# A decoder layer on one core: own tensors in memory for each gated tile, the first half of the merged values kept on chip, residual rows asked for later, the two steps of a norm set apart

## The chip, the core and the metric

The kernel runs on one core of a Trainium2 chip. The core has a matrix engine (PE, with its weight loads shown as PEld), three engines for elementwise work (DVE, ACT, POOL), a queue engine SP that does nothing but ask for transfers, and 16 DMA engines that move the bytes. POOL asks for some transfers too; SP's and POOL's requests go through two different queues (q1 and q0 of the profile). Each engine works its own list of instructions in order and waits at an instruction until everything that it needs is there. The metric is device time in microseconds (us) of one execution; the profile's span runs from the first to the last instruction.

## The reference

One step of a decoder layer over 1024 prompt tokens and 8 sample tokens, in float32. Cut to what matters:

```
def swiglu_half(x, g, w_gate, w_up, w_down):
    u = rmsnorm(x, g)
    return x + 0.5 * ((jax.nn.silu(u @ w_gate) * (u @ w_up)) @ w_down)

h = swiglu_half(x, ...)                        # block one, D_MODEL 1024, D_FF 2816
u = rmsnorm(h); z = u @ w_in                   # latent attention, retention, two gates
h = h + w_out(sigmoid(g_A) * (A @ w_branch_att) + sigmoid(g_B) * (B @ w_branch_ret))
h = swiglu_half(h, ...)                        # block two
h = h + sigmoid(rmsnorm(h) @ w_ple_gate) * (p @ w_ple_proj)
```

The value in the bracket that goes into `w_out` is called the merged value below; silu(gate) times up is called the gated value.

## The kernel before

**Tiling.** All activations lie with features on the 128 partitions and tokens along the free axis. The 1032 tokens are cut into two halves (`tp` 0 and 1) of 2 x 258; `lr` names one 258 of a half. Float32 is multiplied as a high and a low part, three matmuls per product (lines 138 to 140, 331 to 334, 378 to 380, 556 to 558). `split` (lines 103 and 104) makes the parts: a cast on ACT, a subtraction on DVE. KT = 8 is the number of feature tiles of D_MODEL, NF = 22 that of D_FF.

**Stages in order of time.** Block one: norm, gate and up products (to 478 us), down product (493 to 754). Then retention and gates, attention (to 1512). Then the merge: 32 units of 12 matmuls (`proj`, lines 138 to 140), one per feature tile, half and `lr`. Then the out product (`product`, wm times wout). Then block two with the same code as block one (its down product from 2153), and the final part.

**The gated values.** `Block.run` computes gated tiles; `put` splits them and writes each to the memory tensor `mid_d[f, tp]` (SP, line 535; 22 tiles for each half). At the end `fetch` (line 691) asks for the 22 tiles of the first half back from POOL's queue, later for those of the second half from SP's. `product` then runs over the 22 tiles, eight banks at once, 24 matmuls a tile. The rows `h` of the residual stream (line 699, 1032 KB) are added to the product's result when a pass over the 22 tiles is over; that of the first pass is asked for on POOL's queue, the others on SP's. Weight slices `wd` come through SP (line 311).

**The norm.** `rstd2` sums squares with small matmuls over the partitions (line 349), takes a reciprocal root in three rounds on DVE (line 351 and lines 143 to 147, results `sv`, `st`, `sz`), yields, then spreads the result over the partitions (matmuls of line 358, copy to `r` in line 360). At the start of a block `run` asks for four pairs of gate and up products (`plain`, lines 556 to 558); the norm of a half is done between the gate product and the up product of its first pair.

**The merge.** Each unit multiplies its product with a gate `sg` (line 1436), adds the other branch `mr` (line 1437), splits the sum into `mst`, and after two units SP writes 516 KB of `mst` to `mg_d[o, tp]` (line 1442). `sg` and `mr` are asked for five units ahead (line 1417). At unit 20 the code opens the list of wout slices (`Rows`, line 311, 128 KB a slice), asks for the eight merged tiles of the first half back as `wm` (`operand(0)`, line 1403) and for that half's rows of the residual `ht` (`residual(0)`, line 1407, two loads of 1032 KB). After the first group of the out product come `operand(1)` and `residual(1)` for the second half. Results go out through line 1465.

**What sets the order.** The code's own order is not the final one: a planner sorts the instructions of each engine when the program is built, and each waits for what it needs, so that a load can stand earlier on its queue than its line suggests. The rows under "The change" show the final lists.

Of the kernel before, what the change touches and what calls it, by code (L numbers as in the profile page):

```python
# [10 lines left out]
F32 = mybir.dt.float32  # L11
F32R = mybir.dt.float32r
# [8 lines left out]
P = 128  # L21
D = 1024
KT = D // P
# [6 lines left out]
NF = DFF // P  # L30
# [26 lines left out]
def body(ctx, tc, a):  # L57
# [27 lines left out]
    act.copy(warm, ones[:, 0:1])  # L85
    G_QA, G_KVA, G_RET = 5 * KT, 5 * KT + 2, 5 * KT + 3

    hs_d = drp.tile([P, KT, T], F32, name="hs_d")
    h2_d = drp.tile([P, KT, T], F32, name="h2_d")
    h3_d = drp.tile([P, KT, T], F32, name="h3_d")  # L90
    mid1_d = drp.tile([NF, 2, P, 2, 2 * HC], F32, name="mid1_d")
    mid2_d = drp.tile([NF, 2, P, 2, 2 * HC], F32, name="mid2_d")
    ms_d = drp.tile([KT, P, T], F32, name="ms_d")
    ga_d = drp.tile([KT, P, T], F32, name="ga_d")
    u1_d = drp.tile([KT, P, 2, 2 * HC], F32, name="u1_d")
    u2_d = drp.tile([KT, P, 2, 2 * HC], F32, name="u2_d")
    mg_d = drp.tile([KT, 2, P, 2, 2 * HC], F32, name="mg_d")
    vs_d = drp.tile([NB, RH * RD], F32, name="vs_d")


# [142 lines left out]
    def both(tp):  # L243
        return slice(2 * tp * HC, 2 * tp * HC + 2 * HC)

    class Stream:
# [26 lines left out]
        def make(self, units):  # L273
            r = self.load(*units[0])
            self.early(r)
            for i in range(len(units)):
                nxt = None
                for q, part in zip(ORDER, ("a11", "s1", "a11", "a12", "a21", "a12", "a22")):
                    yield self.split(r[part])
                    if q == 0:  # L280
                        dve.tensor_tensor(r["a11"], r["s1"], r["a11"], op=ALU.subtract)
                        if i + 1 < len(units):
                            nxt = self.load(*units[i + 1])
                    elif q == 3:
                        dve.tensor_tensor(r["a12"], r["a12"], r["a11"], op=ALU.subtract)
                    elif q == 6 and nxt:
                        self.early(nxt)
                r = nxt

        def take(self):  # L290
            while len(self.ready) <= self.ahead:
# [130 lines left out]
    class Block:  # L422
# [100 lines left out]
        def run(self, nxt, nxt_st, prepare, accs=None, load=None, more=None):  # L523
# [38 lines left out]
                return self.pe.tile([P, HC], F32, tag="p", name="p")  # L562

            for n, (l, tp) in enumerate(((0, 0), (1, 0), (1, 1), (0, 1))):
                if n == 0 and not begun:
                    rows.ahead, ws, pg = 0, [], []
                    for lr in range(2):
                        load(0, lr)
                        self.fresh(0, lr)
                        ws += [rows.take() for _ in range(2)]  # L570
                        pg.append(plain(ws[:2], 0, lr))
                    load(1, None)
                    squared(0)
                    rows.ahead = 3
                else:
                    if n != 2:
                        ws = [rows.take() for _ in range(4)]
                    pg = [plain(ws[:2], tp, lr) for lr in range(2)]
                if n in (0, 2) and accs[tp] is not None:
                    for _ in self.norm(tp, accs[tp]):  # L580
                        pass
                pu = [plain(ws[2:], tp, lr) for lr in range(2)]
                ts = []
                for lr in range(2):
                    t = pt()
                    ts.append(t)
                    dve.tensor_tensor(t, pg[lr][:, :HC], self.r[tp][:, HV[lr]], op=ALU.mult)
                    act.activation(t, t, AF.Silu)
                for lr in range(2):
                    dve.tensor_tensor(ts[lr], pu[lr][:, :HC], ts[lr], op=ALU.mult)  # L590
                    put(0, tp, l, lr, ts[lr])
                if n == 0:
                    if not begun:
                        squared(1)
                    for _ in self.plain_tokens(1):
                        pass
                elif n == 1:
                    if not begun:
                        self.scaled(0)
                        for _ in self.sums(0):  # L600
                            pass
                    self.last_sum(0)
                elif n == 2:
                    for _ in self.sums(1):
                        pass
# [83 lines left out]
            def fetch(tp, f):  # L689
                mids[tp, f] = t = mp.tile([P, 2, 2 * HC], F32R, tag="m", name="m")  # L690
                self.loaded = (sp if tp else pool).dma_start(t.bitcast(F32), self.mid_d[f, tp])
# [3 lines left out]
            with pools(pre + "h", 2) as hp, pools(pre + "t", 2) as tmp:  # L695
                for tp in TPS:
                    for o in range(2):
                        ht = hp.tile([P, 4, 2 * HC], F32, tag="h", name="h")
                        (sp if tp or o else pool).dma_start(ht, self.src[:, 4 * o:4 * o + 4, both(tp)])
                        end = tp == 1 and o == 1  # L700
                        if end:
                            next(nxt.norms[0])
                        banks = product(rows, lambda f: mids[tp, f], NF, 4,
                                        (lambda f: fetch(1, f)) if (tp, o) == (0, 1) else None)
                        if tp == 1 and o == 0:
                            with tc.issue_after(self.loaded.ins):
                                nxt.first = prepare(nxt.ring)
                        if end:
                            m_st.close()
                            nxt.open_u(nxt_st)  # L710
                            nxt.fetch()
                            next(nxt.norms[0])
                        for n in range(8):
                            hv = ht[:, n // 2, HV[n % 2]]
                            t = tmp.tile([P, HC], F32, tag="c", name="c")
                            dve.scalar_tensor_tensor(t, banks[n][:, :HC], 0.5, self.r[tp][:, HV[n % 2]],
                                                     op0=ALU.mult, op1=ALU.mult)
                            dve.tensor_tensor(hv, hv, t, op=ALU.add)
                            if n % 2:
                                k = 4 * o + n // 2  # L720
                                sp.dma_start(self.dst[:, k:k + 1, both(tp)], ht[:, n // 2:n // 2 + 1])
                        if tp == 1 and o == 0:
                            held = ht
                        if end:
                            for k in range(4):
                                nxt.row(tmp, 1, k, held[:, k])
                        for k in range(4):
                            if tp == 0 or end:
                                nxt.row(tmp, tp, 4 * o + k, ht[:, k])
                        for k in range(4):  # L730
                            nxt.squares(tmp, tp, 4 * o + k, ht[:, k], dve if end else pool)
                        if end and more:
                            more()
# [663 lines left out]
    wms = [wm_st.enter_context(pools("wm0", KT))]  # L1397
    xs = {}

    def operand(tp):  # L1400
        for f in range(KT):
            xs[tp, f] = t = wms[tp].tile([P, 2, 2 * HC], F32R, tag="wm", name="wm")
            sp.dma_start(t.bitcast(F32), mg_d[f, tp])

    def residual(tp):
        for k in range(0, KT, 4):
# [2 lines left out]
    with pools("mt", 2) as mt:  # L1409
# [14 lines left out]
        for j, (tp, o, lr) in enumerate(todo):  # L1424
            if j + 5 < len(todo):
                fetch(*todo[j + 5])
            if j == 20:
                rows = Rows(two.wp, two.rawp, [a["wout"][f][:, o_ * 256:o_ * 256 + 256]
                                               for _ in TPS for o_ in range(4) for f in range(KT)], 3)
                operand(0)  # L1430
                residual(0)
            sg, mr = gates.pop((tp, o, lr))
            ps = bank()
            proj(ps[:, :HC], wa[o // 2], oat, cols(tp, lr), off=(o % 2) * 512)
            m = mt.tile([P, HC], F32, tag="m", name="m")
            dve.tensor_tensor(m, ps[:, :HC], sg, op=ALU.mult)
            dve.tensor_tensor(m, m, mr, op=ALU.add)
            if lr == 0:
                st = mt.tile([P, 2, 2 * HC], F32R, tag="mst", name="mst", bufs=4)
            split(st[:, 0, HV[lr]], st[:, 1, HV[lr]], m)  # L1440
            if lr == 1:
                sp.dma_start(mg_d[o, tp], st.bitcast(F32))
    oat_st.close()
    ring_st.close()

# [4 lines left out]
    for tp in TPS:  # L1450
        sums_of.append(two.accs())
        for o in range(4):
# [2 lines left out]
                    next(steps, None)  # L1455
            banks = product(rows, lambda f: xs[tp, f], KT, 2, each)
            if tp == 0 and o == 0:
                operand(1)
                residual(1)
            for n in range(4):  # L1460
                k = 2 * o + n // 2
# [231 lines left out]
```

## Time and profile before

| what | us |
|---|---|
| three runs, median (lowest to highest) | 2559.3 (2559.25 to 2562.37) |
| the profiled execution's own time | 2556.08 |
| its span | 2553.4 |
| PE busy in the span | 2455.3 (96%) |
| PE's wait ahead of block one's down product | 14.4 |
| PE's wait ahead of block two's down product | 14.6 |
| PE's wait for the norm of block one's second half | 5.4 |
| PE's waits between 1557 and 1612 us, merge and out product | 23.1 |

PE is busy nearly all the time, so the table is to be read from the waits: each line below the fourth is a place where PE stood still, and the line of the code that it stood before is given in the views that are shown with the prediction. The PEclk column there is the mean clock that PE was granted, 1.00 being full.

### The profile page before, as it was taken

The numbers are of one execution on the slowest core, as the hardware profiler recorded it, in microseconds if no ns is written. First come the engines' busy times: TensorE is split into PE (matmuls) and PEld (weight loads), VectorE is DVE, ScalarE is ACT, GpSimd is POOL, SyncE is SP. The second block draws the span as 40 slices with busy tenths as digits, with TensorE's granted clock in tenths as the row PEclk, the third lists the DMA queues.
The fourth block names the chain that finished last, engine by engine and source line by source line (L and its number), as shares of the span: only waits on it lengthen the run. The fifth ranks groups of instructions, "written<-read, shape, count | busy, mean of one in ns | idle before, by whom it ended". The sixth has DMA issues, their size and how long they took to land.

```text
span 2553.4 us, 48889 instructions
## 1 busy us (share of the span) xinstructions
PE 2455.3 (96%) x19132; PEld 2364.0 (93%) x19132; DVE 1473.8 (58%) x3408; ACT 959.8 (38%) x2099; POOL 184.4 (7%) x247
## 2 busy tenths in 40 slices
PE   7999999799999999999999998899999997999998
PEld 7999999799999999999976677899999997999997
DVE  8767667533534666422567774676676675344345
ACT  7444444322322112211245552454444443233221
POOL 0000000111001101110142100000000001110011
PEclk9999999899999999999999998899999998999999
DMA  4323233759622122222134349543232337596231
GB/s 163 104 84 117 103 107 125 268 210 323 206 102 82 56 68 81 82 81 88 38 99 123 113 129 348 184 133 104 84 117 98 111 125 265 204 326 205 92 121 67
DMA packets 176168, 353.15 MB, mean 138 GB/s; under 512 B 19337, under 2 KB 69922, under 8 KB 175938
## 3 DMA queue, kind: packets, MB, share of 16 engines
q1 hardware_dynamic: 163938, 311.08, 36.1%
q0 software_dynamic: 12000, 38.96, 4.1%
q8 instruction: 150, 2.46, 0.4%
q14 instruction: 80, 0.66, 0.1%
HBM read 257.11 MB, written 91.80 MB: 137 GB/s over the span
## 4 chain that ended last, share of the span: by engine, by line
PE 89%; DMA 4%; DVE 4%; issue 1%; ACT 1%; SPq 1%; POOLq 0%; POOL 0%; DVEq 0%; ACTq 0%
PE ps L333 11%; PE ps L331 10%; PE ps L334 10%; PE ps L378 8%; PE ps L379 7%; PE ps L380 7%; PE ps L138 7%; PE ps L139 7%; PE ps L140 7%; PE ps L1186 2%; PE ps L1211 1%; PE ps L1222 1%; PE ps L556 1%; PE ps L557 1%; PE ps L558 1%
## 5 line engine op out<-in xcount | busy, mean ns | idle before, releaser
L333 PE MATMUL ps<-b,w 128*128 128x258 f32 x2240 | 636.6, 284 | 0.0
L331 PE MATMUL ps<-b,w 128*128 128x258 f32 x2240 | 633.1, 283 | 0.0
L334 PE MATMUL ps<-b,w 128*128 128x258 f32 x2240 | 630.2, 281 | 0.0
L378 PE MATMUL ps<-m,w 128*128 128x258 f32 x1408 | 402.6, 286 | 30.7 <-DMA m<-mid_d 29.1
L334 PEld LDWEIGHTS ps<-b,w 128*128 128x128 f32 x2240 | 427.0, 191 | 0.0
L333 PEld LDWEIGHTS ps<-b,w 128*128 128x128 f32 x2240 | 424.8, 190 | 0.0
L331 PEld LDWEIGHTS ps<-b,w 128*128 128x128 f32 x2240 | 421.5, 188 | 0.0
L379 PE MATMUL ps<-m,w 128*128 128x258 f32 x1408 | 399.4, 284 | 0.0
L380 PE MATMUL ps<-m,w 128*128 128x258 f32 x1408 | 398.7, 283 | 0.0
L104 DVE TENSOR_TENSOR w<-wd,w 128x512 fp32r<-128x512 f32 (+1 forms) x264 | 164.8, 637 | 300.1 <-ACT w L103 286.0
L138 PE MATMUL ps<-u,w 128*128 128x344 f32 (+4 forms) x960 | 311.9, 325 | 2.7 <-DMA u<-u_d 2.7
L139 PE MATMUL ps<-u,w 128*128 128x344 f32 (+4 forms) x960 | 308.1, 321 | 0.0
L140 PE MATMUL ps<-u,w 128*128 128x344 f32 (+4 forms) x960 | 307.6, 320 | 0.0
L378 PEld LDWEIGHTS ps<-m,w 128*128 128x128 f32 x1408 | 267.8, 190 | 32.5 <-issue 14.8
L103 ACT CAST w<-wd 128x512 fp32r<-128x512 f32 (+1 forms) x264 | 147.8, 566 | 365.1 <-PE ps L380 325.1
L379 PEld LDWEIGHTS ps<-m,w 128*128 128x128 f32 x1408 | 269.2, 191 | 0.0
L380 PEld LDWEIGHTS ps<-m,w 128*128 128x128 f32 x1408 | 268.1, 191 | 0.0
L104 DVE TENSOR_TENSOR w<-wq,w 128x512 fp32r<-128x512 f32 x264 | 181.5, 689 | 147.9 <-ACT w L103 145.6
L138 PEld LDWEIGHTS ps<-u,w 128*128 128x128 f32 (+1 forms) x960 | 180.1, 188 | 5.4 <-DVE u L413 2.7
L139 PEld LDWEIGHTS ps<-u,w 128*128 128x128 f32 (+1 forms) x960 | 179.5, 187 | 0.9 <-issue 0.4
L140 PEld LDWEIGHTS ps<-u,w 128*128 128x128 f32 (+1 forms) x960 | 179.7, 187 | 0.6
L103 ACT CAST w<-wq 128x512 fp32r<-128x512 f32 x264 | 163.5, 620 | 32.4 <-PE ps L334 23.6
(320 smaller groups left out, 4163.9 us busy)
## 6 DMA issues: line engine op xcount, KB each, us to landing
mid_d<-s SPq DMA_DIRECT2D x88, 516.0 KB, 3.6
m<-mid_d POOLq DMA_DIRECT2D x44, 516.0 KB, 12.3
m<-mid_d SPq DMA_DIRECT2D x44, 516.0 KB, 4.7
wd<-in_f1down_dram SPq DMA_DIRECT2D x88, 256.0 KB, 5.0
wd<-in_f2down_dram SPq DMA_DIRECT2D x88, 256.0 KB, 3.8
ct<-in_cache_dram SPq DMA_DIRECT2D x128, 128.0 KB, 2.1
wq<-in_f1gate_dram SPq DMA_DIRECT2D x44, 256.0 KB, 4.5
wq<-in_f1up_dram SPq DMA_DIRECT2D x44, 256.0 KB, 2.6
```

The lines of the kernel that those rows point to most:

```text
L103: act.copy(dst_hi, src)
L104: dve.tensor_tensor(dst_lo, src, dst_hi.bitcast(F32), op=ALU.subtract)
L138: pe.matmul(ps, w[:, 0, ws], x[:, 0, xs], start=start, stop=False)
L139: pe.matmul(ps, w[:, 0, ws], x[:, 1, xs], start=False, stop=False)
L140: pe.matmul(ps, w[:, 1, ws], x[:, 0, xs], start=False, stop=stop)
L331: pe.matmul(ps, w[:, 0, js], t[:, 0], start=q in (0, 1, 3) and j == 0, stop=False, skip_group_check=True)
L333: pe.matmul(ps, w[:, 0, js], t[:, 1], start=False, stop=False, skip_group_check=True)
L334: pe.matmul(ps, w[:, 1, js], t[:, 0], start=False, stop=j == kh - 1, skip_group_check=True)
L378: pe.matmul(ps, w[:, 0, ws], t[:, 0, HV[n % 2]], start=f == 0, stop=False)
L379: pe.matmul(ps, w[:, 0, ws], t[:, 1, HV[n % 2]], start=False, stop=False)
L380: pe.matmul(ps, w[:, 1, ws], t[:, 0, HV[n % 2]], start=False, stop=f == nf - 1)
L1186: pe.matmul(ps[:, :w], qc[hd][:, i * P:(i + 1) * P], kc[hd][:, j:j + w], start=True, stop=not diag)
```

## The change

Four edits:

- Each gated tile has its own tensor in memory (`halves`, 44 tensors for each block) in place of one tensor for all.
- The rows `h` are all asked for on SP's queue, in the code from inside the product (at its fifth tile).
- The merged values of the first half are split directly into the `wm` tiles that the out product reads; they are no longer written to memory and read back. Only the second half's eight tiles go through memory, each in its own tensor. The wout list is opened at unit 16; at units 25, 27, 29 and 31 one more slice is split ahead (`ahead_one`); `residual(0)` stands behind the merge loop.
- In the first four pairs the norm's first step (sums and root) and its second (spreading) are set apart: for the second half the sums now stand ahead of the gate product, and the spreading always behind the up product.

```
-    mid1_d = drp.tile([NF, 2, P, 2, 2 * HC], F32, name="mid1_d")
+    def halves(name, n):
+        return {(i, tp): drp.tile([P, 2, 2 * HC], F32, name=f"{name}{i}_{tp}") for i in range(n) for tp in range(2)}
+    mid1_d = halves("mid1_d", NF)
...
-    mg_d = drp.tile([KT, 2, P, 2, 2 * HC], F32, name="mg_d")
+    mg_d = [drp.tile([P, 2, 2 * HC], F32, name=f"mg_d{i}") for i in range(KT)]
...
+        def ahead_one(self):
+            self.ready.append(next(self.made))
...
+                norm = None
+                if n == 2 and accs[tp] is not None:
+                    norm = self.norm(tp, accs[tp])
+                    next(norm)
...
-                if n in (0, 2) and accs[tp] is not None:
-                    for _ in self.norm(tp, accs[tp]):
-                        pass
+                if n == 0 and accs[tp] is not None:
+                    norm = self.norm(tp, accs[tp])
+                    next(norm)
                 pu = [plain(ws[2:], tp, lr) for lr in range(2)]
+                if norm:
+                    next(norm)
...
-                        (sp if tp or o else pool).dma_start(ht, self.src[:, 4 * o:4 * o + 4, both(tp)])
+                        def each(f):
+                            if f == 4:
+                                sp.dma_start(ht, self.src[:, 4 * o:4 * o + 4, both(tp)])
+                            if (tp, o) == (0, 1):
+                                fetch(1, f)
...
-            if j == 20:
+            if j == 16:
                 rows = Rows(two.wp, two.rawp, [a["wout"][f][:, o_ * 256:o_ * 256 + 256]
                                                for _ in TPS for o_ in range(4) for f in range(KT)], 3)
-                operand(0)
-                residual(0)
+            elif j > 24 and j % 2:
+                rows.ahead_one()
...
             if lr == 0:
-                st = mt.tile([P, 2, 2 * HC], F32R, tag="mst", name="mst", bufs=4)
+                if tp == 0:
+                    xs[0, o] = st = wms[0].tile([P, 2, 2 * HC], F32R, tag="wm", name="wm")
+                else:
+                    st = mt.tile([P, 2, 2 * HC], F32R, tag="mst", name="mst", bufs=4)
             split(st[:, 0, HV[lr]], st[:, 1, HV[lr]], m)
-            if lr == 1:
-                sp.dma_start(mg_d[o, tp], st.bitcast(F32))
+            if tp == 1 and lr == 1:
+                sp.dma_start(mg_d[o], st.bitcast(F32))
+    residual(0)
```

**SP at the start of block one's down product.** Line 535 (541 in the changed kernel) writes gated tiles, line 699 (714) asks for `h`, line 311 (317) for weight slices. Before:

```order
51 L311 DMA wd<-in_f1down_dram 128x512 x13
52 L535 DMA mid_d<-s 128x1032 x2
53 L311 DMA wd<-in_f1down_dram 128x512
54 L699 DMA h<-in_xT_dram 128x4x516
55 L311 DMA wd<-in_f1down_dram 128x512 x20
```

Now:

```order
81 L317 DMA wd<-in_f1down_dram 128x512 x13
82 L541 DMA mid_d_0_114<-s 128x1032
83 L541 DMA mid_d_0_116<-s 128x1032
84 L714 DMA h<-in_xT_dram 128x4x516
85 L317 DMA wd<-in_f1down_dram 128x512
86 L714 DMA h<-in_xT_dram 128x4x516
87 L317 DMA wd<-in_f1down_dram 128x512 x20
```

Both `h` loads of the first half now stand on SP right behind the last two writes of gated tiles, though the code has them at the fifth tile.

**POOL at the same place.** The fetches of gated tiles are line 691 (703); what each waits for is in brackets, DMAHW being SP's requests. Before:

```order
6 L699 DMA h<-in_xT_dram 128x4x516 [waits DMAHW5_49,DMAHW4_49,DMAHW6_49,DMAHW3_49,DMAHW7_49,DMAHW0_49,DVE_49]
7 L691 DMA m<-mid_d 128x1032 [waits DMAHW4_49,DMAHW5_49,DMAHW2_49,DMAHW6_49,DMAHW1_49,DMAHW0_49]
8 L691 DMA m<-mid_d 128x1032 [waits DMAHW7_49,DMAHW3_49,PE_49]
9 L691 DMA m<-mid_d 128x1032 x3
```

Now:

```order
6 L703 DMA m<-mid_d_0_74 128x1032 [waits DMAHW3_49,DMAHW4_49,DMAHW2_49,DMAHW5_49,DMAHW1_49,DMAHW6_49,DMAHW0_49,DVE_49]
7 L703 DMA m<-mid_d_0_76 128x1032 [waits DMAHW7_49,PE_49]
8 L703 DMA m<-mid_d_0_78 128x1032
```

`h` is gone from the head of POOL's list. The first fetch still waits for the same writes of SP as before, among them that of gated tile 20 (DMAHW1), and now also for the DVE row that ended that tile.

**SP behind the merge.** Line 1442 (1462) writes merged tiles, 1403 (1420) fetches them, 1407 (1424) loads the residual, 1465 (1486) writes results, 311 (317) loads wout slices. Before:

```order
798 L1442 DMA mg_d<-mst 128x1032 x3
799 L311 DMA wd<-in_wout_dram 128x256 x6
800 L1403 DMA wm<-mg_d 128x1032 x8
801 L1407 DMA ht<-hs_d 128x4x516 x2
802 L1465 DMA h_d<-ht 128x516 x2
803 L311 DMA wd<-in_wout_dram 128x256 x15
```

Now:

```order
825 L1462 DMA mg_d_173<-mst 128x1032
826 L1424 DMA ht<-hs_d 128x4x516
827 L317 DMA wd<-in_wout_dram 128x256 x6
828 L1420 DMA wm<-mg_d_166 128x1032
...
835 L1420 DMA wm<-mg_d_173 128x1032
836 L1424 DMA ht<-hs_d 128x4x516 x2
837 L1486 DMA h_d<-ht 128x516 x2
838 L317 DMA wd<-in_wout_dram 128x256 x15
```

The list behind the last write is the same but for one load of residual rows (1032 KB) ahead of it. The other load of the first half's residual stands among the gate loads of the merge.

**The norm of block one's second half.** On PE the sums move from row 247 to row 175; the spreading stays in row 344:

```order
247 L349 MATMUL ps_653<-ones,acc 128x1 x6
...
344 L358 MATMUL ps_674<-ident,sz 128x128 x2
```

```order
175 L355 MATMUL ps_696<-ones,acc 128x1 x6
...
344 L364 MATMUL ps_817<-ident,sz 128x128 x2
```

DVE's first and last row of the root stand at 67 and 87 in both, with the same rows between them (`sz` in row 87: line 147, now 150).

More of the change, by code (lines that the diff above doesn't have):

```diff
@@ L90, in body @@
     h3_d = drp.tile([P, KT, T], F32, name="h3_d")
-    mid1_d = drp.tile([NF, 2, P, 2, 2 * HC], F32, name="mid1_d")
-    mid2_d = drp.tile([NF, 2, P, 2, 2 * HC], F32, name="mid2_d")
+    mid1_d = halves("mid1_d", NF)
+    mid2_d = halves("mid2_d", NF)
     ms_d = drp.tile([KT, P, T], F32, name="ms_d")
@@ L702, in run @@
                             next(nxt.norms[0])
-                        banks = product(rows, lambda f: mids[tp, f], NF, 4,
-                                        (lambda f: fetch(1, f)) if (tp, o) == (0, 1) else None)
+                        banks = product(rows, lambda f: mids[tp, f], NF, 4, each)
                         if tp == 1 and o == 0:
@@ L1398, in body, with operand @@
     xs = {}
-    def operand(tp):
+    def operand():
         for f in range(KT):
-            xs[tp, f] = t = wms[tp].tile([P, 2, 2 * HC], F32R, tag="wm", name="wm")
-            sp.dma_start(t.bitcast(F32), mg_d[f, tp])
+            xs[1, f] = t = wms[1].tile([P, 2, 2 * HC], F32R, tag="wm", name="wm")
+            sp.dma_start(t.bitcast(F32), mg_d[f])
     def residual(tp):
@@ L1457, in body @@
             if tp == 0 and o == 0:
-                operand(1)
+                operand()
                 residual(1)
```

## The prediction

> **What bounds the kernel now.** I read the page first, for the share of each engine and the chain that ended last.
>
> ```profile
> PE 2455.3 (96%) x19132; PEld 2364.0 (93%) x19132; DVE 1473.8 (58%) x3408; ACT 959.8 (38%) x2099; POOL 184.4 (7%) x247
> ...
> PE 89%; DMA 4%; DVE 4%; issue 1%; ACT 1%; SPq 1%; POOLq 0%; POOL 0%; DVEq 0%; ACTq 0%
> ...
> L378 PE MATMUL ps<-m,w 128*128 128x258 f32 x1408 | 402.6, 286 | 30.7 <-DMA m<-mid_d 29.1
> ```
>
> PE works 96% of the span and the change takes no matmul away. So a gain can only come from PE's waits, and the last row names the largest: 29.1 us ahead of line 378 for a tile `m` from memory. The view of waits, taken around the two down products, shows that these are two waits of one kind:
>
> ```profile
> PE ps L378 <- DMA m<-mid_d: 14.4, 1, 14.4
> ...
> PE ps L378 <- DMA m<-mid_d: 14.6, 1, 14.6
> ```
>
> The change also touches the norm (5.4 us) and the merge; I take the three places in turn.
>
> **Part 1, the two starts of a down product.** The timeline of SP's and POOL's requests at the first of them (start, length, queue, line):
>
> ```profile
> 479.58 1.27 SPq L535 DMA_DIRECT2D mid_d<-s  x2
> 480.90 0.72 SPq L311 DMA_DIRECT2D wd<-in_f1down_dram  x1
> 481.67 1.17 SPq L699 DMA_DIRECT2D h<-in_xT_dram  x1
> ...
> 480.81 0.91 POOL L699 DMA_DIRECT2D h<-in_xT_dram  x1 [480.33 <-DVE s L104]
> 484.47 3.67 POOL L691 DMA_DIRECT2D m<-mid_d  x7 [2.75 <-DMA mid_d<-s]
> 491.00 0.53 POOL L691 DMA_DIRECT2D m<-mid_d  x1 [2.87 <-DMA h<-in_xT_dram]
> 493.04 0.53 POOL L691 DMA_DIRECT2D m<-mid_d  x1 [1.51 <-DMA m<-mid_d]
> ```
>
> POOL asks for `h` at 480.8, waits 2.75 us for the write of gated tile 20, asked for at 479.6, and asks for the first `m` at 484.5. The two rows below it tell when things land, because POOL's ninth request waits for its first: `h` at 490.9, the first `m` 2 us later, at 492.9, when PE starts. So the first `m` comes behind 1032 KB of `h` on POOL's queue. The wait itself stays after the change: the fetch still waits for the write of tile 20, so own tensors alone are worth 0. What goes is `h` from POOL's queue; both `h` now stand on SP's, and their bytes are in the air all the same. The window behind the wait (length, then busy time and count of PE, PEld, DVE, ACT, POOL; last PEclk, DMA share, GB/s):
>
> ```profile
> 493.00:497.00 4.00, 4.00 (x20) 4.00 (x21) 0.00 (x0) 0.00 (x0) 1.58 (x3) 0.53 1.03 412
> ```
>
> The view of DMA from 484 to 490 us shows the two queues at work together (MB and share of the 16 engines), and its row of a lone write in the merge the time of 516 KB on a nearly free queue:
>
> ```profile
> DMA packets 689, 2.01 MB, mean 336 GB/s; under 512 B 42, under 2 KB 42, under 8 KB 689
> ...
> q0 software_dynamic: 331, 1.30, 62.4%
> q1 hardware_dynamic: 358, 0.71, 35.1%
> ...
> mg_d<-mst SPq DMA_DIRECT2D x1, 516.0 KB, 2.9
> ```
>
> POOL's queue got 1.30 MB in 6 us, 0.217 MB a us, so 516 KB (0.528 MB) take 2.4 us there. A lone write of that size takes 2.9 us to land, of which 1.3 is transfer at the 412 GB/s that these engines reach in that window; 1.6 is left as fixed. Together 4.0 us from request to landing. The request comes at about 483.6 in place of 484.5: the write of tile 20 let POOL go on 4.9 us after it was asked for, with POOL's `h` in the air from 480.8 on; it takes something between the lone 2.9 and that without it. So the first `m` lands at about 487.6, not 492.9: **5.2 us** gained. Bounds: alone in the air, 2.9 us after a request at 483.1, 6.9 us; behind both `h`, a loss, which is a rival below; with no earlier request and half as much share, 484.5 + 1.6 + 4.8 = 490.9, 2.0 us. I take 5.0, nearer the share that POOL's queue was seen to get. The next tiles come every 2.4 us and PE needs one in 24 x 0.12 = 2.9 us, so no new wait follows; the weights wait today too. The window behind the wait shows 20 matmuls in 4 us at a clock of 0.53, where 34 would fit, 1.7 us lost. That stays, since 9 us of wait are left. Block two has the same rows with a wait of 14.6. Sum of part 1: **10 us**, 4 to 13.
>
> The Trainium skill, "DMA: Bandwidth & Descriptors", section "Queues, rings and completion order", says that each DMA engine takes turns between the queues that have work, packet by packet. This case's shares of 62 and 35% are not equal turns by time, though both queues do move at once. By equal turns the first `m` would get 0.168 MB a us, land 0.7 us later, and the sum of this part would be 8.6.
>
> **Part 2, the norm.** The sums (line 349) and the spreading (line 358) on PE, DVE's first and last step of the root, and the busy time of the engines in between:
>
> ```profile
> 45.91 1.40 PE L349 MATMUL ps<-ones,acc 128*128 128x1 f32 x12
> ...
> 64.36 2.72 PE L358 MATMUL ps<-ident,sz 128*128 128x128 f32 x12 [5.37 <-DVE sz L147]
> ```
>
> ```profile
> 53.57 0.17 DVE L351 TENSOR_SCALAR sv<-ps 128x6 f32<-128x6 f32 x1
> ...
> 64.14 0.17 DVE L147 SCALAR_TENSOR_TENSOR sz<-st,sz 128x6 f32<-128x6 f32 x1
> ```
>
> ```profile
> 47.00:59.00 12.00, 11.98 (x99) 11.78 (x98) 12.00 (x18) 4.91 (x7) 0.00 (x0) 1.00 0.34 111
> 59.00:64.30 5.30, 0.00 (x0) 0.00 (x0) 5.30 (x11) 2.38 (x4) 0.00 (x0) 0.90 0.00 0
> ```
>
> The sums are there at 47.3, and DVE takes them up only at 53.57: it is busy for the whole of both stretches, 12.00 and 5.30 us (the third of the busy times), working through its list. The sums come 72 rows sooner on PE, 72 x 0.12 = 8.6 us, but DVE's list up to the end of the root is the same, without idle time in it, so `sz` is ready at 64.3 as before. PE has the same rows ahead of the spreading. Gain **0**. Above, if DVE were free after all, the whole wait of 5.4 and about 2.5 of clock; below, a few DVE rows behind the root (0.4 to 0.7 us each) trade places, up to 2 us.
>
> **Part 3, the merge.** The view of waits on PE from 1557 to 1612, and the windows of that stage (columns as above):
>
> ```profile
> PE ps L378 <- ACT w L103: 12.3, 2, 11.8
> PE ps L138 <- DVE m L1436: 7.9, 1, 7.9
> PE ps L378 <- DMA wm<-mg_d: 2.9, 5, 0.7
> ```
>
> ```profile
> 1540.00:1557.00 17.00, 16.74 (x136) 16.33 (x135) 11.77 (x31) 4.25 (x11) 0.00 (x0) 1.00 0.99 333
> 1557.00:1565.00 8.00, 4.78 (x21) 3.17 (x19) 0.00 (x0) 0.00 (x0) 0.00 (x0) 0.79 1.02 412
> 1572.50:1579.00 6.50, 6.42 (x30) 6.43 (x31) 4.94 (x14) 1.63 (x4) 0.00 (x0) 0.52 1.01 363
> ```
>
> Up to 1557 PE does 30 of the 32 units with hardly a wait. Then the eight `wm` of the first half stand on SP ahead of the last gates: PE has four small waits and one of 7.9 us, and the rest runs at half clock. PE starts and ends here, and the list of SP behind the merge:
>
> ```profile
> 1512.33 0.39 PE L138 MATMUL ps<-oa,w 128*128 128x258 f32 x1
> ...
> 1557.32 0.36 PE L378 MATMUL ps<-wm,w 128*128 128x258 f32 x1
> ...
> 1608.99 0.58 PE L378 MATMUL ps<-wm,w 128*128 128x258 f32 x1 [11.76 <-ACT w L103]
> ```
>
> ```profile
> 1576.70 5.49 SPq L1442 DMA_DIRECT2D mg_d<-mst  x3
> 1582.24 3.18 SPq L311 DMA_DIRECT2D wd<-in_wout_dram  x6
> 1585.47 5.48 SPq L1403 DMA_DIRECT2D wm<-mg_d  x8
> 1591.42 1.62 SPq L1407 DMA_DIRECT2D ht<-hs_d  x2
> 1594.06 4.48 SPq L1465 DMA_DIRECT2D h_d<-ht  x2
> 1598.63 13.50 SPq L311 DMA_DIRECT2D wd<-in_wout_dram  x14
> ```
>
> The second wait, 11.8 us, is for the fifteenth wout slice. It stands on SP behind everything that the last merged write lets go: six slices, eight `wm`, two `ht`, two writes, 7.8 MB in all; from the last write (1582.2) to PE's start (1609.0) it is a chain of 26.8 us, 0.29 MB a us. After the change that list is the same but for 1032 KB (1.06 MB) more ahead, 1.06 / 0.29 = 3.6 us at this mean rate, 2.6 at 412 GB/s: I add 3.0. The chain begins when the last merged write is issued. The units need 45.0 us for 30, so 48.0 for 32: PE ends the merge at 1560.3. Before, PE ended it by 1578 and the last write was out at 1582.2, 4 us behind; with DVE in full work I take 3.5 now, 1563.8. Then PE goes on with slice 15 at 1563.8 + 26.8 + 3.0 = 1593.6 in place of 1609.0: **15.4 us**. PE would reach that slice at 1560.3 + 14 x 1.43 = 1580.3, so a wait of 13 us stays in the same place: the two waits become one, and only the first is won. That the eight writes and fetches of the first half are gone (16 x 516 KB) does not count beside this; it is what lets the units run through. Bounds: the last write at 1561 and 2.6 for the extra load give 18.6; above a second half that is held to 333 GB/s (its gates and writes, 516 KB a unit and thus 1.6 us a unit, end at 1563, last write at 1568 with a backlog, 3.6 for the load), 10.6. The slices split ahead cost DVE and ACT some 0.4 us each and end before they are needed.
>
> **Sum.** 10 + 0 + 15.4 = 25 us: the profiled execution's 2556.1 becomes 2531, and the median of the runs, 3.2 us above that execution, 2534.
>
> **Rivals.**
>
> *All waits go.* If own tensors and the on-chip half did away with each wait they touch: 14.4 + 14.6 + 5.4 + 23.1 = 57 us, and some 2 us of half clock at each of five places, 10: 2559 - 67 = 2492. For it, nothing in the lists of requests; against it, the fetch still waits for tile 20 and slice 15 still stands last. 4%.
>
> *The first `m` gains nothing.* `h` of SP's queue takes its place in the air; part 1 is 0 to 3 us and 2559 - 17 = 2542 is left. For it: both `h` are asked for some 2 us ahead. Against: POOL's 62%. 15%.
>
> *The merge gains little.* The DMA share is 0.99 in the merge, and if the second half's gates come late the last write is not out before 1572; with the extra load part 3 is 7 us: 2559 - 17 = 2542 too. For it, 0.99; against it, PE's 16.74 of 17 us busy at that share, and no writes in the first half. 12%.
>
> *Slower: the DMA engines serve in the order of asking, and bytes set the pace in all three places.* SP's `h` at 481.67 needed 14.0 us:
>
> ```profile
> h<-in_xT_dram SPq DMA_DIRECT2D x1, 1032.0 KB, 14.0
> ```
>
> The first `m` would then land behind it, at 495.7 + 1.6 = 497.3, 4.4 us later than now, twice 8.8. The merge, on this view, pays 3 us for the extra load and gains only what it moves less. It decides from a gain below 12 in part 3: with none the time is 2559 + 12 = 2571. Against it: on POOL's queue the first `m` landed while SP's older `h` was still in the air. 4%.
>
> *The change does nothing that counts* (the planner's lists differ but the chains keep their length): within 0.2%. 3%.
>
> My own case has the remaining 62%. The range that holds 8 in 10 takes in the bounds of both parts and the two cases at 2542: **2523 to 2547**; my case alone is 2527 to 2541. A measurement of this kernel tells about 0.2% (5 us). Faster by more than that: 0.92; within it 0.04; slower 0.04.
>
> **What would show it.** In the changed profile: PE's waits ahead of both down products near 9.4 us, not 14.5, with POOL's first request an `m` at about 483.6; the wait for `sz` still at 5.4 (line 364); no wait of PE for line 1453, the merge in one run to 1560, and one wait of about 13 us for slice 15, ending near 1589, 20 us earlier than before (all of the trace from 493 on stands 5 us earlier for part 1, so the merge ends at 1555). I am wrong if the first `m` lands behind `h` again, or if the last merged write is out later than 1565.

## The result, and the profile after

The changed kernel takes 2541.97 us (median; 2538.61 to 2543.56) against 2560.84 (2559.25 to 2564.43) before: a ratio of 0.9923, 95% interval 0.9905 to 0.994. Timed once more in another set of runs it stood at 0.9914 (0.9901 to 0.9928). It is faster by about 0.8%, 19 to 21 us in the medians of the two sets; the forecast was 25. The profiled execution's span is 2540.8 us, 12.6 us shorter than the one before, and less than the times say; where the difference went is told below.

The waits of PE at the places of the change, in the order of the prediction: both down products, the norm, and the stage from the merge to the out product.

```profile
PE ps L384 <- DMA m<-mid_d: 12.9, 1, 12.9
...
PE ps L384 <- DMA m<-mid_d: 13.3, 1, 13.3
...
PE ps L364 <- DVE sz L150: 6.6, 1, 6.6
...
PE ps L384 <- ACT w L106: 12.1, 1, 12.1
```

The two waits ahead of the down products were 14.4 and 14.6 and fell by 1.5 and 1.3 us in this profile, where 5 each were forecast. The norm's wait grew from 5.4 to 6.6. In the merge one wait is left, for the fifteenth wout slice, and the four small ones and that of 7.9 us are gone, as the prediction had it.

The merge in the timeline of PE (its first matmul, its last with the first of the out product, the end of the wait) and SP's list behind it:

```profile
1518.22 0.39 PE L141 MATMUL ps<-oa,w 128*128 128x258 f32 x1
...
1564.64 0.28 PE L143 MATMUL ps<-oa,w 128*128 128x258 f32 x1
1564.75 0.28 PE L384 MATMUL ps<-wm,w 128*128 128x258 f32 x1
...
1597.92 0.58 PE L384 MATMUL ps<-wm,w 128*128 128x258 f32 x1 [12.15 <-ACT w L106]
```

```profile
1563.78 4.91 SPq L1462 DMA_DIRECT2D mg_d<-mst  x3
1568.74 0.43 SPq L1424 DMA_DIRECT2D ht<-hs_d  x1
1569.22 3.94 SPq L317 DMA_DIRECT2D wd<-in_wout_dram  x6
1573.20 6.90 SPq L1420 DMA_DIRECT2D wm<-mg_d  x8
1580.87 1.60 SPq L1424 DMA_DIRECT2D ht<-hs_d  x2
1583.42 3.67 SPq L1486 DMA_DIRECT2D h_d<-ht  x2
1587.18 14.97 SPq L317 DMA_DIRECT2D wd<-in_wout_dram  x15
```

From the merge's first matmul to the end of the wait for slice 15 the kernel before took 1608.99 - 1512.33 = 96.7 us; the changed one takes 1597.92 - 1518.22 = 79.7, 17.0 less. While the merge's units run, PE hardly stands still, at less than full use of the DMA engines (length, busy time and count of PE, PEld, DVE, ACT, POOL; PEclk, DMA share, GB/s):

```profile
1517.00:1540.00 23.00, 23.00 (x196) 22.69 (x197) 20.41 (x50) 11.11 (x24) 0.00 (x0) 1.00 0.87 262
1540.00:1560.00 20.00, 20.00 (x169) 20.00 (x169) 16.06 (x44) 5.65 (x14) 0.00 (x0) 1.00 0.93 300
```

The units run through at 46.5 us for 32, 1.45 each, the last write is issued 4.0 us after the last unit, and the chain from there to slice 15 is 29.2 us, as worked out (29.8).

But the merge began at 1518.2, 5.9 us later than in the profile before, although the first down product started 0.6 us earlier. That loss lies in attention, of which the change touches no row. The windows of that stage, before and then after (columns as above):

```profile
1322.00:1337.00 15.00, 15.00 (x73) 9.02 (x71) 6.12 (x18) 4.43 (x15) 7.76 (x8) 0.77 0.54 154
1337.00:1350.00 13.00, 12.05 (x113) 8.02 (x112) 8.28 (x29) 7.74 (x25) 1.90 (x2) 1.00 0.32 94
```

```profile
1322.00:1337.00 15.00, 15.00 (x65) 9.43 (x63) 3.98 (x12) 3.41 (x11) 7.44 (x8) 0.54 0.54 146
1337.00:1350.00 13.00, 11.09 (x77) 5.40 (x75) 8.22 (x28) 4.61 (x14) 1.91 (x2) 1.00 0.37 103
```

From 1322 to 1337 PE was granted 0.77 of its clock before and 0.54 after, and it is 44 matmuls behind by 1350. So the profile leaves three questions: why the down products won so little, why the norm's wait grew, and whether attention's loss belongs to the change.

### The profile page after: what moved, and what is told of

Its sections match the earlier page's. It is cut to its first block, busy times and chain, and to the rows that moved or that the text cites. A ratio compares the mean times of both kernels' runs of the same rounds, so it can differ in the third digit from the quotient of the medians.

```text
span 2540.8 us, 48866 instructions
## 1 busy us (share of the span) xinstructions
PE 2453.4 (97%) x19132; PEld 2361.3 (93%) x19132; DVE 1471.0 (58%) x3408; ACT 958.7 (38%) x2099; POOL 183.2 (7%) x245
## 4 chain that ended last, share of the span: by engine, by line
PE 55%; DMA 2%; DVE 1%; issue 0%; ACT 0%; SPq 0%; POOLq 0%; POOL 0%; DVEq 0%; ACTq 0%
PE ps L141 5%; PE ps L142 5%; PE ps L143 5%; PE ps L339 5%; PE ps L337 5%; PE ps L340 5%; PE ps L384 4%; PE ps L385 4%; PE ps L386 4%; PE ps L1203 2%; PE ps L1228 2%; PE ps L1239 2%; PE ps L563 1%; PE ps L562 1%; PE ps L564 1%; PE ps L1351 1%
## 5 line engine op out<-in xcount | busy, mean ns | idle before, releaser
L384 PEld LDWEIGHTS ps<-m,w 128*128 128x128 f32 x1408 | 267.6, 190 | 29.6 <-issue 13.4
```

The source lines that it names most:

```text
L384: pe.matmul(ps, w[:, 0, ws], t[:, 0, HV[n % 2]], start=f == 0, stop=False)
```

## The experiments

All times below are medians, and each ratio is against the kernel before in the same set of runs. "The changed kernel" is at 2537 us, 0.9914; it was timed in the first of three sets only, with the runs "Attention once more", both runs on the rows `h` and the first run on the list behind the merge. The kernel before stood at 2557.84, 2557.76 and 2561.57 us in the three sets, so a difference from 2537 in the other two sets is good to some 4 us, and the ratio is the better guide.

**Attention once more.** The changed kernel again, and the kernel before again.

> The changed kernel once more, for the attention stage, which took 6.5 us more in its profile than before the change though no row of it moved: half clock for 13.65 us there, not 6.83. Theory 'chance': the clock's two more windows at half are drawn anew in each execution; this profile then shows 6.83 or 13.65 us of half clock behind 1322, and PE ends attention near 1511 or near 1517, each as likely. Theory 'cause': the change shifts the stage against the clock's windows by 0.35 us and so always costs it; then 13.65 us and 1517 again. The two waits ahead of the down products stay at 12.9 and 13.3, the wait for slice 15 at 12.2, the norm's at 6.6.

> The kernel before, once more, for the attention stage alone: 197.9 us in its first profile with 6.8 us of half clock behind the stall at 1318; the changed kernels, with the same rows in that stage, took from 198.0 (6.8 us of half clock) to 204.1 (13.7). If the length is drawn anew in each execution, this one lies anywhere from 198 to 204, in step with its half clock; if the change costs it, it is 198 again.

The changed kernel again: 2536.95 us. Its attention stage took 200.9 us from its first product to the merge's first, between the 197.9 of the first profile before and the 204.1 of the first profile after, with 13.7 us of half clock (a granted clock of 0.50). Neither expectation was met as stated: 13.7 us of half clock were to go with 1517, and the stage ended at 1514.9. Nor did the waits ahead of the down products stay at 12.9 and 13.3:

```profile
PE ps L384 <- DMA m<-mid_d: 13.6, 1, 13.6
...
PE ps L384 <- DMA m<-mid_d: 13.8, 1, 13.8
```

The kernel before again, in one execution of 2560.43 us, with the same two windows:

```profile
1322.00:1337.00 15.00, 15.00 (x64) 9.49 (x63) 3.99 (x12) 3.29 (x11) 7.29 (x8) 0.54 0.48 141
1337.00:1350.00 13.00, 11.02 (x77) 5.61 (x77) 8.13 (x28) 4.85 (x14) 1.90 (x2) 1.00 0.35 102
```

That is the profile of after, on the kernel of before: 0.54 of the clock, 77 matmuls, and a stage of 203.7 us. Over all 13 profiles of this study the stage lies between 197.9 and 204.1, with the change and without it. The length is drawn anew in each execution and the loss isn't the change's; the first profile before was a short draw and the first after a long one. The half clock seems to have a part in it and isn't all: the stage took 197.9 to 201.0 us with 6.8 us of half clock, 198.9 to 202.9 with 10.2, 200.9 to 204.1 with 13.7, and 202.1 with 17.1. What else makes it longer stays open.

**The rows `h` back on POOL's queue.** One edit of the change undone, own tensors kept:

```
-                            if f == 4:
-                                sp.dma_start(ht, self.src[:, 4 * o:4 * o + 4, both(tp)])
...
+                        (sp if tp or o else pool).dma_start(ht, self.src[:, 4 * o:4 * o + 4, both(tp)])
```

> The changed kernel with one edit undone: the rows h of the first pass are asked for on POOL's queue again, from outside the product. Own tensors stay. If only the place of h made the difference of 1.5 us at each down product, both waits are 14.4 to 14.6 again and the time is 3 us longer than the changed kernel's. If own tensors gave something, the waits stay below 14.

2540.82 us, 0.9933 (0.9919 to 0.9946), 3.9 us above the changed kernel. The waits ahead of the down products:

```profile
PE ps L384 <- DMA m<-mid_d: 15.0, 1, 15.0
...
PE ps L384 <- DMA m<-mid_d: 14.9, 1, 14.9
```

Own tensors gave nothing here: the waits are no shorter than before the change (14.4 and 14.6, then 14.6 and 13.9 in the second profile of that kernel). What the place of `h` gave is small, and a single profile does not tell it: in the six profiles with the changed kernel's requests the waits are 12.9 to 13.9 and 12.9 to 14.5, 13.5 and 13.7 on average, against 14.5 and 14.3 on average before. That is 1.6 us for both; the time says 3.9 against this run. What is left of the change, in the main the merge and the norm, is worth 17 us in time (2557.84 - 2540.82).

**The rows `h` out of the way.** Both loads of the first half behind the 22 fetches, on the same queue (`last0` is the 22nd fetch):

```
-                            if f == 4:
+                            if f == 4 and tp == 0:
+                                with tc.issue_after(self.last0.ins):
+                                    pool.dma_start(ht, self.src[:, 4 * o:4 * o + 4, both(tp)])
+                            elif f == 4:
                                 sp.dma_start(ht, self.src[:, 4 * o:4 * o + 4, both(tp)])
```

> The changed kernel with both h loads of the first half asked for on POOL behind the 22 fetches of gated tiles, so that nothing but the last writes and one weight slice is in the air when the first fetch is asked for. In the changed kernel POOL's queue moved no byte for 3.4 us after that fetch was asked for, while SP's queue moved the h rows. Theory 'backlog': the engines work off what SP has asked for first; then the dead time goes, the first tile lands 3 to 3.5 us after its request and both waits fall to 9 to 9.5, 7 us gained in all. Theory 'lead time': POOL's request takes 3 to 3.7 us to its first byte whatever else is in the air; then only the sharing goes, the tile lands 5 to 5.5 us after its request, the waits are 11 to 11.5, 3 to 4 us gained in all.

2530.59 us, 0.989 (0.9875 to 0.9905), 6.4 below the changed kernel. The request and PE's start in its timelines:

```profile
484.48 0.69 POOL L703 DMA_DIRECT2D m<-mid_d  x1 [484.01 <-DMA mid_d<-s]
...
488.25 0.58 PE L384 MATMUL ps<-m,w 128*128 128x258 f32 x1 [9.75 <-DMA m<-mid_d]
```

It is 3.8 us from request to landing, with waits of 9.75 and 9.87 us. In the changed kernel it was 6.8 us. The views of DMA there, from the request (485.4) to 489, and from 489.5 to 491 (queue: packets, MB, share of the engines):

```profile
DMA packets 639, 1.27 MB, mean 352 GB/s; under 512 B 25, under 2 KB 25, under 8 KB 639
...
q1 hardware_dynamic: 639, 1.27, 98.3%
...
DMA packets 202, 0.62 MB, mean 411 GB/s; under 512 B 1, under 2 KB 1, under 8 KB 202
...
q0 software_dynamic: 98, 0.40, 65.5%
q1 hardware_dynamic: 104, 0.21, 36.7%
```

For 3.7 us SP's queue had the engines and POOL's moved nothing; then they shared. With `h` gone POOL's first packet came 1.4 us after the request. So "backlog" is the nearer theory, a little outside its figures (3 to 3.5 us to landing, 9 to 9.5 us of wait): 3.0 us of the 6.8 went, 2.3 of them ahead of the first packet.

The profile before the change has the same stretch. POOL's `h`, asked for at 480.8, ahead of SP's, moved nothing until 484.0; from 482.5 to 484 the only queue at work was SP's:

```profile
q1 hardware_dynamic: 128, 0.45, 98.1%
```

**Another order of the gated tiles.** Tiles 1 to 21, then 0, in the fetches, the product and its weights (whose list is turned in the same way). The fixed tags keep each tile in the place that it had; what changes is the order alone:

```
-            mp = m_st.enter_context(pools(pre + "m", NF, side="right"))
+            mp = m_st.enter_context(pools(pre + "m", side="right"))
...
+            turn = lambda f: (f + 1) % NF
+            for f in (0, *range(NF - 1, 0, -1)):
+                mids[0, f] = mp.tile([P, 2, 2 * HC], F32R, tag=f"m{f}", name="m")
             for f in range(NF):
-                fetch(0, f)
+                pool.dma_start(mids[0, turn(f)].bitcast(F32), self.mid_d[turn(f), 0])
...
-                        banks = product(rows, lambda f: mids[tp, f], NF, 4, each)
+                        banks = product(rows, lambda f: mids[tp, turn(f)], NF, 4, each)
```

> The changed kernel with the 22 gated tiles taken in another order: 1 to 21, then 0, in the fetches, the product and its weights, and each tile with a fixed place. Tile 0's place in SBUF is that of the buffer out of which gated tile 20 is written, and it was the first in POOL's list, so that all others stood behind that write; the places of tiles 1 to 4 have been free for long. Theory 'place': the wait ahead of each down product is the first fetch's wait for that place, the way and the bytes in the air; with tiles 1 to 4 fetched during block one's last products it goes from 13.5 to under 2 us, and the time falls by 20 to 28 us to about 2512. Rival 'next wait': PE then waits for something else that is late by the same 10 us, the banks' evacuation or the fetches from tile 5 on behind h; then less than 12 us are gained and the profile names it.

2511.3 us, 0.9822 (0.9808 to 0.9835), 25.7 below the changed kernel, 23.5 by the ratios. POOL's fetches and PE up to the end of block one:

```profile
77.08 0.69 POOL L709 DMA_DIRECT2D m<-mid_d  x1 [76.60 <-DVE b L107]
117.17 0.54 POOL L709 DMA_DIRECT2D m<-mid_d  x1 [39.40 <-DMA mid_d<-s]
120.93 0.53 POOL L709 DMA_DIRECT2D m<-mid_d  x1 [3.22 <-DMA mid_d<-s]
159.10 0.53 POOL L709 DMA_DIRECT2D m<-mid_d  x1 [37.64 <-DMA mid_d<-s]
459.68 4.76 POOL L709 DMA_DIRECT2D m<-mid_d  x9 [300.05 <-PE ps L340]
...
482.14 0.28 PE L340 MATMUL ps<-b,w 128*128 128x258 f32 x1
482.27 0.28 PE L384 MATMUL ps<-m,w 128*128 128x258 f32 x1
```

Tiles 1 to 4 are now fetched by 160 us, nine more are asked for from 22 us before the block's end on, and the down product follows the block's last product with no wait at all; what is left of waits near 480 is 1.6, 0.7 and 0.3 us. "Place" held: the wait was the first fetch's wait for a buffer out of which a later tile was still written, with that fetch's own time to landing behind it, and all other fetches queued behind it, though the places of four had long been free.

**The norm's steps together again.**

```
-                norm = None
-                if n == 2 and accs[tp] is not None:
-                    norm = self.norm(tp, accs[tp])
-                    next(norm)
...
-                if n == 0 and accs[tp] is not None:
-                    norm = self.norm(tp, accs[tp])
-                    next(norm)
+                if n in (0, 2) and accs[tp] is not None:
+                    for _ in self.norm(tp, accs[tp]):
+                        pass
...
-                if norm:
-                    next(norm)
```

> The changed kernel with the norm's two steps together again, as before the change. In all profiles of the changed norm the wait for sz is 6.6 us, before the change it was 5.4. Theory 'earlier sums cost': the sums' earlier place pushes rows on DVE ahead of the root back or forth, and with the old code the wait is 5.4 again, 1 to 1.5 us less in the first 66 us; too little for the whole time, which stays within 2 us of the changed kernel's 2537. Rival 'chance': 6.6 is drawn by the start of the execution and stays with the old code.

2537.45 us, 0.9919 (0.9906 to 0.9933): no difference in time. The wait for `sz` is 5.4 again (5.3 or 5.4 in each profile with the old order), and 6.6 in each with the new. But it is not a loss of its own. PE's waits from 26 to 45 us with the old order, and then in the changed kernel:

```profile
PE ps L364 <- DVE sz L150: 1.1, 1, 1.1
PE ps L563 <- DVE b L107: 0.8, 1, 0.8
PE ps L562 <- ACT w L106: 0.4, 1, 0.4
PE ps L562 <- DVE p L593: 0.3, 1, 0.3
```

```profile
PE ps L364 <- DVE sz L150: 1.1, 1, 1.1
PE ps L562 <- DVE p L599: 0.3, 1, 0.3
PE ps L562 <- ACT w L106: 0.2, 1, 0.2
```

With the sums earlier, two waits of 1.2 us together shrink to 0.2. Counted from the first half's spreading (29.2 and 30.9), PE comes to the second half's after 28.4 us in place of 29.6, and that spreading starts after 35.0 us in both: PE is 1.2 us earlier and waits 1.2 us longer for a DVE that is no earlier.

**The list behind the merge.** Three runs on the wait for slice 15. First, the second half's fetches behind the second group of the out product:

```
-            if tp == 0 and o == 0:
+            if tp == 0 and o == 1:
                 operand()
                 residual(1)
```

> The changed kernel with the fetch of the second half's merged tiles and residual rows put behind the second group of the out product, not the first, so that SP asks for wout slices 15 to 22 ahead of those 6.3 MB. Theory 'list': the wait of 12.2 us for slice 15 is nothing but SP's list; it goes below 1 us, at most 4 us come back at slice 23, and the time falls by 9 to 12 us. Rival 'moved on': the list is as long as before, and PE waits for slice 23 nearly as long as now for slice 15, so that less than 3 us are gained.

2533.78 us, 0.9905 (0.989 to 0.9921), 3.2 below the changed kernel. PE's one wait of that stage, and its place:

```profile
1599.76 0.58 PE L384 MATMUL ps<-wm,w 128*128 128x258 f32 x1 [7.88 <-ACT w L106]
```

No wait is left at slice 15, but 7.9 us come back at slice 23, the first that stands behind the 6.3 MB now. Neither expectation was met: 4 us of the wait of 12 went, and the time fell by no more. Second, only the 4.2 MB of merged tiles there, the 2.1 MB of residual rows behind the fourth group:

```
-            if tp == 0 and o == 0:
+            if tp == 0 and o == 1:
                 operand()
+            if tp == 0 and o == 3:
                 residual(1)
```

> The changed kernel with the second half's merged tiles fetched behind the second group of the out product and its residual rows behind the fourth. With both behind the second group PE waited 7.9 us for slice 23; the residual rows are 2.1 MB, 5.4 us at the 0.39 MB a us of that stretch. Theory 'list': the wait at slice 23 falls to 2.5 us, at most 4, and the time is 5 to 9 us below the changed kernel's 2537. Rival: the wait is set by when the list begins, not by its length, and stays above 6.

2532.23 us, 0.9887 (0.9872 to 0.9902), 4.7 below the changed kernel, 6.9 by the ratios, where 5 to 9 were expected:

```profile
PE ps L384 <- ACT w L106: 2.8, 1, 2.8
```

The wait fell by 5.1 us, near the 5.4 that were worked out for the rows taken out of the list: it is the list's length. The profile shows the gain in the stage too, 81.2 us from the merge's start to slice 23 against 86.1; in time the two runs are not clearly apart (0.9887 and 0.9905, with intervals that overlap). Third, the same transfers on POOL's idle queue in place of SP's:

```
-            sp.dma_start(t.bitcast(F32), mg_d[f])
+            pool.dma_start(t.bitcast(F32), mg_d[f])
...
-            sp.dma_start(two.hts[tp][:, k:k + 4], hs_d[:, k:k + 4, both(tp)])
+            (pool if tp else sp).dma_start(two.hts[tp][:, k:k + 4], hs_d[:, k:k + 4, both(tp)])
```

> The changed kernel with the second half's merged tiles and residual rows asked for on POOL's queue, which has nothing to do there, and not on SP's. SP's list behind the last merged write is then one residual load and wout slices. Theory 'list': no wait above 1 us is left at any wout slice, and the time falls by 11 to 15 us from the changed kernel's 2537. Rival: the bytes (6.3 MB) hold the slices up in the air as they did in SP's list; by turns the slices still come at half rate, so that at most 3 us of the 12 stay.

2538.65 us, 0.9926 (0.9912 to 0.9939), no better than the changed kernel. The wait came earlier, at slice 9, and was 10.0 us. DMA from 1564.9, when SP asked for slices, to 1581.5:

```profile
DMA packets 2173, 6.36 MB, mean 383 GB/s; under 512 B 167, under 2 KB 448, under 8 KB 2172
...
q0 software_dynamic: 1191, 4.48, 71.3%
q1 hardware_dynamic: 981, 1.87, 29.6%
...
wd<-in_wout_dram SPq DMA_DIRECT2D x8, 128.0 KB, 18.8
```

A slice of 128 KB took 18.8 us to land (the median of eight), beside the 4.5 MB of the other queue and behind 1032 KB of residual rows on its own. A queue of its own was no way around bytes that are asked for too early; asking for them later brought a part of the wait back. This run fell to the rival, and more than it had said: 10 us of wait stayed, not 3.

**Two that were put together.** The turned order with the POOL queue:

> The last two edits together, the version to beat both kernels. If they are independent, the gains add: about 2500, from 2494 to 2506. If PE's clock or the transfers of one place spoil the other, it is above 2506.

2512.4 us, 0.9822 (0.9808 to 0.9835): the first edit's gain alone, as the second had none; the 2500 that was expected is missed. And the turned order with the late fetches and the old norm, the three edits above with no line changed:

> The gated tiles in turned order, the fetches of the second half late as in the run beside this one, and the norm's steps together as before the change. If the gains add, 2511 less 5 to 9 less 1: 2502 to 2506. If the out product's wait only moves, 2509 or more.

2506.99 us, 0.9785 (0.9772 to 0.9799): 30 us below the changed kernel (33 by the ratios) and 2.1% below the one before, a little above the 2502 to 2506 that were expected. Its one wait in the out product is

```profile
PE ps L384 <- ACT w L106: 2.5, 1, 2.5
```

The profiled execution drew a long attention stage, 202.9 us.

## Why the prediction was right, and where it was not

The range of 2523 to 2547 held the 2541.97, and direction and the larger part were right. The size, 25 us against 19 to 21, was too large, and it is as near as it is by luck in part: part 1 gave some 6 to 8 us less than forecast and part 3 some 2 to 5 us more.

**Part 3, 15.4 us in the sum, was right in mechanism and near in size.** The merge runs through in one piece, the wait for slice 15 stays, and SP's list is the chain to it. Between the merge's start and the end of that wait 17.0 us went (79.7 against 96.7), and 19.9 in the second pair of profiles (78.1 against 98.0), the latter above the bound of 18.6. The unit took 1.45 us, not 1.50, and the wait that is left was 12.1, not 13. The last merged write was issued at 1568.7, later than the 1565 that was to prove the prediction wrong; but the merge began 5.9 us later in that profile by attention's draw, and from the merge's start it is 50.5 us where 51.5 were worked out. The late-fetch runs show that this wait is the list's length: 2.1 MB out of it, 5.1 us out of the wait. With the norm at nothing and the rows `h` at 2 to 4 us, the 17 us that are left in time are the merge's; how much each of its edits gives (the half kept on chip, the list opened earlier, the slices split ahead) no run separates.

**Part 1, 10 us in the sum, was mis-sized: it measured 2 to 4** (1.6 by the mean waits, 2.8 in the first pair of profiles, 3.9 by time against the run with `h` on POOL's queue). That own tensors alone are worth nothing, and that the wait for the write of tile 20 stays, held. The term that failed is the 4.0 us from request to landing: it measured 6.8. It was made of 1.6 us fixed, from a lone write on SP's queue, and 2.4 us at the share that POOL's queue had been seen to get. But the shares of 62 and 35% were read from 484 on, when both queues were under way; that POOL's queue had moved nothing in the 3 us ahead of that, while SP's had the engines, stood in the same profile and went into no term. Now both `h` are asked for some 3.5 and 1.5 us before the first `m`, and SP's queue had the engines alone for another 3.7 us after its request.

The second term, a request 0.9 us earlier, failed as well. Counted from the moment PE stops, the request comes after 6.1 us before and after the change. 6.1 and 6.8 make the 12.9 us of wait.

Without that backlog the term measured 3.8 us, and the waits were 9.75 and 9.87, close to the 9.4 of the prediction. That is chance: 4.0 was worked out for a shared road, and by the same pieces a free one would have taken 2.9, the prediction's own bound. The rival "the first `m` gains nothing", put at 15%, is the one that came nearest: 0 to 3 us for part 1, `h` of SP's queue in the place of POOL's in the air, and a time of 2542. The sign that was to prove the prediction wrong, that the first `m` lands behind `h` again, came true in substance: SP's queue moved 1.27 MB after the request before the first byte of `m`.

The Trainium skill's rule of turns between the queues, packet by packet ("DMA: Bandwidth & Descriptors", "Queues, rings and completion order"), is borne out once both queues move: 98 packets on POOL's and 104 on SP's from 489.5 to 491, of unlike size, so that POOL's got 0.40 MB of 0.62. The prediction held the shares of 62 and 35% against that rule, but they are shares of time: the packets of its view, 331 and 358, are nearly equal turns too. No run here shows whether that rule says anything of the 3.7 us ahead of it, in which one queue had everything.

**Part 2, 0, was right,** for the reason given: DVE's list to the end of the root is what PE waits for. That PE would come to it 1.2 us earlier, and wait that much longer, was not foreseen; the wait was to stay at 5.4.

**The rivals.** "All waits go" is out: with the changed lists the waits ahead of the down products and of slice 15 stayed. "Slower" and "nothing that counts" are out by the time. "The merge gains little" is out: DMA's share was 0.87 in the first half, with no writes, and 0.93 in the next 20 us, and PE was busy throughout.

**What the prediction did not look at** is the place of the first buffer. It took the wait for tile 20's write as given, and the waits of 29 us that begin with it are the largest of the kernel: turning the order of the tiles takes 23.5 to 25.7 us off, as much as the whole forecast.

## What to carry to other kernels

When a load was moved to another queue here, its bytes still went over the same engines: count what is asked for ahead of the transfer that someone waits for, on every queue, and ask for the rest later. In an in-order queue, look at what the first request waits for: here the first fetch's place was in use until the end of the block, those of the next four had been free by 160 us, and all 21 others stood behind the first. And before a stage's loss is put down to a change, look at the same stage in a second profile of the old kernel: here it varied by 6 us by itself.

## What the runs showed of the hardware that was not expected

A transfer asked for on POOL's queue while the two loads of `h` stood on SP's queue moved its first byte only 3.7 us after its request, with 98.3% of the engines' time going to the other queue; with those loads out of the way it was 1.4 us. A 128 KB slice on SP's queue, beside 4.5 MB of POOL's and behind 1032 KB of its own, took 18.8 us. And around one and the same stall of 3.5 us in attention the clock stayed at half for 6.8, 10.2, 13.7 or 17.1 us in different executions; in the two with 13.7 that are shown above, PE was busy throughout from 1322 to 1337.
